# Low parts of the weight tiles: a second ScalarE pass and an adding transfer in place of a VectorE subtraction

## The chip, the core and the metric

The kernel runs on one core of a Trainium2 chip. The core has TensorE (PE; its weight loads are shown as PEld), VectorE (DVE), ScalarE (ACT), GpSimd (POOL) and SyncE (SP), which work side by side and wait for one another through semaphores, and 16 DMA engines that move data between HBM and SBUF. The metric is the device time of one execution in microseconds (us).

## The reference

One inference step of one layer of a hybrid diffusion backbone, in fp32, for 512 latent and 128 context tokens of width 1024. Cut to what matters here:

```python
h = rms_norm(x, norm1_g) * (1.0 + scale1) + shift1
proj = h @ w_in                      # q, k, v, conv, z, x/B/C, dt, gates
y_attn = blocked_attention(...) @ w_attn_o
y_conv = (conv_bg * dwconv_centred(conv_cg * conv_x, conv_w)) @ w_conv_o
y_ssd  = rms_norm(y * silu(z), ssd_norm_g) @ w_ssd_o
out = (g_attn * y_attn + g_conv * y_conv + g_ssd * y_ssd) @ w_merge
x = x + gate1 * out
h = rms_norm(x, norm2_g) * (1.0 + scale2) + shift2
hg, hu = jnp.split(h @ ffn_w1, 2, axis=-1)
x = x + gate2 * ((silu(hg) * hu) @ ffn_w2)
```

Nearly all the arithmetic is products of a token matrix with a weight matrix.

## The kernel before

TensorE multiplies in the rounded format fp32r, which keeps part of an fp32 value. To come close to fp32 every operand X is held as two parts: the high part is X rounded to fp32r, the low part is X minus the high part. A product takes three matmuls: high x high, high x low, low x high.

**Making the parts of a weight tile.** `wraw` (L173) lets SP load up to four blocks of 128 rows by 256 columns, 512 KB, into a raw tile `wr`, of which there are three. `wtiles` (L163) gives a pair `wh`, `wl` out of rings of four each. `split` (L154) then copies the raw tile into `wh` on ACT, which rounds it (L156), and subtracts on DVE, `wl = wr - wh` (L157). A raw tile can be loaded anew when its subtraction is done; `wh` and `wl` can be written anew when TensorE has done its last matmul with the tile that they held before. `wload` (L178) does this for a whole set of 1024 rows in two tiles. Nearly all weight splits are issued with high priority, so that the scheduler of the framework sets them early in the queues of ACT and DVE. Each engine's queue runs in order, as does SP's queue of DMA issues.

**The stages, in order of time.** Start-up and the modulation of the first norm (to 45 us). Attention (45 to 450 us): keys, values and queries by `tblock` (L274), with gate and convolution projections as filling work. Eight groups of the state-space scan (450 to 1043 us): `group_proj` (L746) projects the next group (weights w_x, w_bc, w_z) while `group_scan` (L777) works on the present one; its rows `rw` come back from HBM through SP (L818). The merge of the three branches (1043 to 1270 us): for each pair of 128-column blocks a `wload` of w_ao, w_co or w_so, and `fblock` (L250), 96 matmuls of 320 columns; beside it DVE works off the second modulation (L956), whose rows SP loads. The product with w_mg in two halves of the tokens (L1055), the second norm (`norm_half`, L1080; its power runs on POOL, L282) and the first feed-forward unit by `plain_half` (L1110). From about 1385 us the feed-forward part.

**A feed-forward unit.** `sunit` (L208) computes a 1024 x 256 weight block times the tokens with seven products instead of eight (a Strassen-Winograd scheme). `sload` (L190) loads the block in two raw tiles `r0`, `r1`, forms four sums of quarters on POOL (L197 to L200) in the tiles `ws`, of which there are two, and splits seven quarters into four pairs of `wh`, `wl`. A product is 12 matmuls; between products, ACT copies the first one out of PSUM and DVE adds and subtracts the others (all at L225, through the helper `first`). Twenty such units, two for each column block, alternate with `ff_down` (L1168), which multiplies by the second feed-forward matrix.

**Where the change touches.** `split` stays for the activations and for the narrow w_dt; `wload`, `sload`, `plain_half` (L1113), the load of the first feed-forward unit (L1130), the host's layout of `w_f1` (L1272) and the scratch memory for DMA descriptors (L1285) are changed.

## Time and profile before

| | us |
|---|---|
| three runs, median | 1819.34 |
| three runs, lowest and highest | 1816.97, 1819.56 |
| profiled execution, device time | 1815.66 |
| its span, first to last instruction | 1813.9 |

The profile is of one execution. Its clock of TensorE was granted at 0.993 of full speed over the span. A row of the groups gives line, engine, operation, what it writes and reads (names without buffer numbers), shape and count, then busy time and the mean of one in ns, then the idle time of the engine before these instructions and who ended it. A row of the waits gives who waited for whom: total us, how often, longest. Matmuls overlap each other and the weight loads, so a matmul's own duration (311 ns for 320 columns) is longer than the distance to the next one.

### The profile page before, as it was taken

What the parts mean: (1) busy time and instruction counts of PE and PEld (TensorE: products, weight loads), DVE (VectorE), ACT (ScalarE), POOL (GpSimd) and SP (SyncE); (2) the same over time, 40 slices, a digit from 0 to 9 for tenths busy, and PEclk for the clock granted to TensorE, in tenths of its full rate; (3) what the DMA queues carried; (4) which work ended last, traced back from release to release, by engine and by line L of the source; (5) the groups of instructions that cost most, each with busy time, mean ns of one, the idle gap of its engine ahead of it and who ended that gap; (6) DMA issues with size and microseconds to landing.
All of it is one profiled execution on the core that took longest, in us unless ns stands there. A gap on an engine that the chain in (4) does not pass through costs nothing. (4 is left out here: it accounts for less than half of the span.)

```text
span 1813.9 us, 30158 instructions
## 1 busy us (share of the span) xinstructions
PE 1763.5 (97%) x12104; PEld 1692.3 (93%) x12104; DVE 1203.6 (66%) x2179; ACT 779.6 (43%) x1548; POOL 157.6 (9%) x117
## 2 busy tenths in 40 slices
PE   7999999999999999999999999999988999999999
PEld 3999999999999999999999999999988999999999
DVE  5648545545677677777775478878669666767675
ACT  5554554444455555555555342212345332324240
POOL 0110000000000000000000000000016232232320
PEclk9999999999999999999999999999999999999999
DMA  7312212125243433434334488665531222223222
GB/s 294 108 39 78 69 58 76 68 74 156 75 138 103 144 119 111 140 87 142 119 111 138 131 300 274 216 196 162 190 108 47 82 70 82 74 79 96 67 77 76
DMA packets 110524, 216.50 MB, mean 119 GB/s; under 512 B 9328, under 2 KB 53232, under 8 KB 109360
## 3 DMA queue, kind: packets, MB, share of 16 engines
q1 hardware_dynamic: 110384, 214.58, 36.5%
q8 instruction: 95, 1.56, 0.3%
q14 instruction: 45, 0.37, 0.1%
HBM read 191.05 MB, written 23.49 MB: 118 GB/s over the span
## 5 line engine op out<-in xcount | busy, mean ns | idle before, releaser
L256 PE MATMUL acc<-h,wh 128*128 128x320 f32 x3072 | 582.0, 311 | 3.3 <-DVE s L505 1.0
L256 PEld LDWEIGHTS acc<-h,wh 128*128 128x128 f32 x3072 | 480.7, 188 | 4.7 <-DVE pTl L157 1.6
L157 DVE TENSOR_TENSOR wl<-wr,wh 128x1024 fp32r<-128x1024 f32 (+1 forms) x226 | 279.6, 1238 | 124.9 <-ACT wh L156 115.6
L256 PE MATMUL acc<-h,wl 128*128 128x320 f32 x1536 | 350.4, 309 | 0.9 <-DVE wl L157 0.9
L156 ACT CAST wh<-wr 128x1024 fp32r<-128x1024 f32 (+1 forms) x226 | 224.6, 996 | 282.5 <-PE acc L256 147.4
L256 PE MATMUL acc<-s,wh 128*128 128x320 f32 x1472 | 287.1, 310 | 0.4 <-ACT wh L156 0.4
L256 PEld LDWEIGHTS acc<-h,wl 128*128 128x128 f32 x1536 | 257.0, 188 | 1.4 <-DVE wl L157 1.4
L256 PEld LDWEIGHTS acc<-s,wh 128*128 128x128 f32 x1472 | 234.8, 188 | 1.0 <-ACT wh L156 0.7
L256 PE MATMUL acc<-s,wl 128*128 128x320 f32 x736 | 179.3, 310 | 1.1 <-DVE wl L157 1.1
L246 PE MATMUL mx<-wh,h 128*128 128x256 f32 x560 | 161.6, 289 | 1.7 <-DVE vl L157 1.0
L247 PE MATMUL mx<-wl,h 128*128 128x256 f32 x560 | 159.0, 284 | 0.0
L248 PE MATMUL mx<-wh,h 128*128 128x256 f32 x560 | 158.8, 284 | 0.0
L220 PE MATMUL acc<-s,wh 128*128 128x320 f32 x640 | 148.0, 317 | 5.0 <-ACT s L225 3.0
L256 PEld LDWEIGHTS acc<-s,wl 128*128 128x128 f32 x736 | 126.1, 189 | 2.1 <-DVE wl L157 2.1
L220 PEld LDWEIGHTS acc<-s,wh 128*128 128x128 f32 x640 | 105.6, 188 | 13.1 <-ACT s L225 7.1
L220 PE MATMUL acc<-h,wh 128*128 128x320 f32 x480 | 112.0, 317 | 3.8 <-DVE s L225 2.8
L956 DVE CUSTOM_DVE_ANT_0 jk<-aw,cr 128x512 f32<-128x512 f32 x128 | 88.2, 689 | 34.1 <-DMA aw<-in_ada_dram 32.6
L246 PEld LDWEIGHTS mx<-wh,h 128*128 128x128 f32 x560 | 107.7, 193 | 2.3 <-DVE vl L157 1.2
L825 ACT ACTIVATE ex<-rw,nlc 128x128 f32<-128x128 f32 x320 | 101.8, 391 | 15.4 <-DVE M L827 9.4
L247 PEld LDWEIGHTS mx<-wl,h 128*128 128x128 f32 x560 | 107.9, 193 | 0.0
L248 PEld LDWEIGHTS mx<-wh,h 128*128 128x128 f32 x560 | 107.7, 192 | 0.1
L1052 DVE SCALAR_TENSOR_TENSOR s<-acc,mod,s 128x320 f32<-128x320 f32 (+2 forms) x168 | 65.6, 433 | 61.3 <-PE acc L256 61.1
(267 smaller groups left out, 2612.7 us busy)
## 6 DMA issues: line engine op xcount, KB each, us to landing
wr<-in_w_f_dram SPq DMA_DIRECT2D x64, 512.0 KB, 3.6
rw<-D_a SPq DMA_DIRECT2D x40, 512.0 KB, 5.1
aw<-in_ada_dram SPq DMA_DIRECT2D x64, 256.0 KB, 3.5
wr<-in_w_cv_dram SPq DMA_DIRECT2D x24, 512.0 KB, 3.7
wr<-in_w_gt_dram SPq DMA_DIRECT2D x24, 512.0 KB, 5.0
aw<-in_ada_dram SPq DMA_DIRECT2D x8, 1024.0 KB, 6.7
wr<-in_w_x_dram SPq DMA_DIRECT2D x16, 512.0 KB, 3.9
wr<-in_w_bc_dram SPq DMA_DIRECT2D x16, 512.0 KB, 3.9
```

The source lines that it names most:

```text
L156: act.copy(hi_t, src)
L157: dve.tensor_tensor(lo_t, src, f32(hi_t), op=sub)
L220: pe.matmul(out, y, z, start=not more and i == 0 and j == 0, stop=i == KB // 2 - 1 and j == 2, skip_group_check=True)
L246: pe.matmul(out, l.hi, r.hi, start=start, stop=False)
L247: pe.matmul(out, l.hi, r.lo, start=False, stop=False)
L248: pe.matmul(out, l.lo, r.hi, start=False, stop=stop)
L256: pe.matmul(ps[:, e, :HT], x, y[:, e * HT:(e + 1) * HT], start=first and i == 0 and j == 0, stop=last and i == k - 1 and j == 2)
L825: act.activation(ex[:, d, r, :], rw[:, d, r, :], AF.Exp, bias=nlc[:, c, j:j + 1])
L956: dve.tensor_tensor_reduce(jk, aw, cr[:, s, :], 0.5, 0.0, op0=mult, op1=add, accum_out=mp[:, q, m, s:s + 1])
L1052: dve.scalar_tensor_tensor(dst[:, a:a + n], ps[:, e, a - e * HT:a - e * HT + n], gcol[:, k, s:s + 1], dst[:, a:a + n], op0=mult, op1=add)
```

## The change

A new helper `wsplit` makes both parts of a weight tile: ACT copies the raw tile into `wh` as before, a second ACT pass writes the negative of `wh` into `wl`, and a DMA issued from POOL adds the raw tile onto `wl`. It is used for every weight tile of 256 columns; DVE no longer takes part. The raw tile is read by the DMA, so it comes free when that has landed.

So that the quarters of `w_f1` lie in one piece for the DMA, the host lays that matrix out by quarters, and `sload` and the first feed-forward unit load quarters (`qraw`, `qload`); the numbers in them are the same. The scratch memory for descriptors of DMAs issued by POOL grows from 1024 to 2048.

```diff
+    def wsplit(hi_t, lo_t, src):
+
+        act.copy(hi_t, src)
+        act.mul(lo_t, f32(hi_t), -1.0)
+        pool.dma_start(lo_t, src, accum_op=add)
+
@@ wload
-                split(w.hi, w.lo, raw)
+                (wsplit if n == 256 else split)(w.hi, w.lo, raw)
...
+    def qraw(src, a):
+        t = wp.tile([P, 2, 4, P], F32, tag="wr", name=nm("wr"), bufs=3)
+        nc.sync.dma_start(t, src[:, a])
+        return t
+
+    def qload(src):
+
+        out = []
+        for a in range(2):
+            raw, w = qraw(src, a), wtiles((2, 4, P))
+            with tc.high_priority():
+                wsplit(w.hi, w.lo, raw)
+            out.append(w)
+        return out
+
@@ sload
-        r0, r1 = (wraw(src, a, a + 4).rearrange("p k (m c) -> p m k c", m=2) for a in (0, 4))
+        r0, r1 = qraw(src, 0), qraw(src, 1)
...
-            split(w[0].hi[:, 0], w[0].lo[:, 0], r0[:, 0])
-            split(w[0].hi[:, 1], w[0].lo[:, 1], s24[:, 0])
-            split(w[1].hi, w[1].lo, s31)
-            split(w[2].hi, w[2].lo, r1)
-            split(w[3].hi[:, 0], w[3].lo[:, 0], s24[:, 1])
+            wsplit(w[0].hi[:, 0], w[0].lo[:, 0], r0[:, 0])
+            wsplit(w[0].hi[:, 1], w[0].lo[:, 1], s24[:, 0])
+            wsplit(w[1].hi, w[1].lo, s31)
+            wsplit(w[2].hi, w[2].lo, r1)
+            wsplit(w[3].hi[:, 0], w[3].lo[:, 0], s24[:, 1])
@@ plain_half
-            l, x = w[:, i, m * P:(m + 1) * P], forms[("B11", "B21", "B12", "B22")[2 * e + i // 4]][i % 4]
+            l, x = w[i // 4][:, m, i % 4], forms[("B11", "B21", "B12", "B22")[2 * e + i // 4]][i % 4]
@@ layer_kernel
-    wg, wu = wload(w_f1[0, 0]), wload(w_f1[1, 0])
+    wg, wu = qload(w_f1[0, 0]), qload(w_f1[1, 0])
@@ host
+def _quarters(w):
+
+    t = _wt(w)
+    return t.reshape(*t.shape[:2], 2, 4, 2, P).transpose(0, 1, 2, 4, 3, 5)
...
-        "w_f1": _wt(f1).reshape(2, 11, P, KB, 256),
+        "w_f1": _quarters(f1).reshape(2, 11, P, 2, 2, 4, P),
...
-    nc = bacc.Bacc("TRN2", target_bir_lowering=False, num_devices=1, dynamic_dma_scratch_size=1024)
+    nc = bacc.Bacc("TRN2", target_bir_lowering=False, num_devices=1, dynamic_dma_scratch_size=2048)
```

## The prediction

> **What bounds the kernel now.** I read the page's first two parts, then busy time by stage, then the list of waits.

> ```profile
> span 1813.9 us, 30158 instructions
> PE 1763.5 (97%) x12104; PEld 1692.3 (93%) x12104; DVE 1203.6 (66%) x2179; ACT 779.6 (43%) x1548; POOL 157.6 (9%) x117
> ```

> TensorE is busy 97% of the span: the end is set by the stream of matmuls, and the change leaves their number as it is. What can be won is time in which TensorE stands still for an operand. By stage (columns: stretch, length, busy time and instructions of each engine, granted clock, DMA share, GB/s):

> ```profile
> 0.00:45.00 45.00, 32.24 (x156) 15.61 (x156) 22.62 (x42) 22.46 (x38) 1.38 (x5) 0.92 0.80 296
> 45.00:450.00 405.00, 393.68 (x2871) 385.46 (x2871) 226.49 (x484) 201.76 (x436) 14.35 (x13) 0.99 0.25 80
> 450.00:1043.00 593.00, 593.00 (x4148) 564.38 (x4147) 402.17 (x718) 308.61 (x722) 1.17 (x1) 1.00 0.38 120
> 1043.00:1270.00 227.00, 222.67 (x1509) 220.64 (x1508) 181.31 (x373) 59.09 (x73) 0.00 (x0) 1.00 0.70 230
> 1270.00:1350.00 80.00, 76.85 (x514) 76.31 (x513) 54.49 (x88) 35.94 (x55) 3.12 (x2) 0.98 0.48 161
> 1350.00:1410.00 60.00, 51.52 (x320) 49.02 (x319) 48.07 (x69) 27.92 (x60) 34.70 (x28) 0.94 0.17 49
> 1410.00:1813.90 403.90, 393.51 (x2599) 380.85 (x2597) 268.42 (x407) 123.87 (x168) 102.85 (x68) 1.00 0.25 78
> ```

> The start-up splits no weights before 44.7 us; attention (45 to 450) lacks 11 us, the scan stage (450 to 1043) nothing, the merge of the branches (1043 to 1270) 4, the stage around the second norm 12, the feed-forward part 10. DVE is the fuller helper everywhere from 450 on (80% in the merge, 80% around the norm). Who made TensorE wait (engine, line, who; total us, times, longest):

> ```profile
> PEld acc L220 <- DVE s L225: 8.3, 13, 1.0
> PEld acc L220 <- ACT s L225: 7.1, 19, 0.8
> PEld acc L256 <- DVE wl L157: 3.5, 6, 1.2
> PE acc L220 <- DVE s L225: 4.8, 12, 0.7
> PE acc L220 <- ACT s L225: 3.0, 6, 0.5
> PE acc L256 <- DVE wl L157: 2.0, 4, 0.9
> PEld acc L289 <- POOL rs L282: 6.3, 3, 3.2
> SPq L175 <- DVE wl L157: 971.3, 180, 30.4
> ```

> The first six are the waits that a lighter DVE queue can shorten: the seven-product units of the feed-forward part (L220) wait for subtractions and a copy at L225 that stand in queues behind weight splits, and a few merge tiles wait for the split itself. The loads sum to 8.3 + 7.1 + 3.5 = 18.9 us, the matmuls behind them to 4.8 + 3.0 + 2.0 = 9.8. The gain cannot exceed 19 us, and is near 10 if only what TensorE lost comes back.

> **What is removed and added.** These are the weight splits, by shape:

> ```profile
> L157 DVE TENSOR_TENSOR wl<-wr,wh 128x1024 fp32r<-128x1024 f32 x200 | 258.0, 1291 | 123.9 <-ACT wh L156 114.8 <-PE mx L839 5.5 <-PE acc L620 1.8
> L157 DVE TENSOR_TENSOR wl<-ws,wh 128x512 fp32r<-128x512 f32 x40 | 30.8, 771 | 1.0
> L157 DVE TENSOR_TENSOR wl<-ws,wh 128x1024 fp32r<-128x1024 f32 x20 | 24.5, 1223 | 3.0 <-ACT wh L156 3.0
> L157 DVE TENSOR_TENSOR wl<-wr,wh 128x512 fp32r<-128x512 f32 x24 | 20.8, 866 | 0.0
> L156 ACT CAST wh<-wr 128x1024 fp32r<-128x1024 f32 x200 | 209.0, 1047 | 226.0 <-PE acc L256 124.5 <-issue 30.7 <-PE acc L220 25.8
> L156 ACT CAST wh<-ws 128x512 fp32r<-128x512 f32 x40 | 24.8, 620 | 50.0 <-PE acc L256 24.0 <-PE acc L220 23.9 <-POOL ws L199 2.1
> ```

> DVE loses 258.0 + 30.8 + 24.5 + 20.8 = 334 us (1204 to 870, 48%). ACT gains a second pass, which I price like the first: 220 of 1.05 and 64 of 0.62 = 271 us (780 to 1051, 58%); no stage fills it, the scan stage going from 309 to about 375 of 593 us. POOL gains 284 DMA issues, and the DMA engines 220 x 0.524 + 64 x 0.262 = 132 MB to add. None of these is on the path by its sum. What decides is **latency**: a low part was there 1.2 us after its rounded part; now it comes after a second ACT pass (1.05 us), an issue on POOL and a landing. Call issue plus landing D.

> **The cost D.** No transfer of before is issued by POOL or adds. The nearest rows (size, median us from issue to landing):

> ```profile
> wr<-in_w_f_dram SPq DMA_DIRECT2D x64, 512.0 KB, 3.6
> aw<-in_ada_dram SPq DMA_DIRECT2D x8, 1024.0 KB, 6.7
> wr<-in_w_mg_dram SPq DMA_DIRECT2D x16, 512.0 KB, 4.3
> out_dram<-so SPq DMA_DIRECT2D x8, 256.0 KB, 2.0
> out_dram<-raw SPq DMA_DIRECT2D x1, 128.0 KB, 1.7
> ```

> An addition must read source and destination, so it moves like 1024 KB read. The stores, whose source is SBUF as here, go from 1.7 to 2.0 us for 128 KB more: 0.3 per 128 KB after 1.4, hence 2.6 for 512 KB read once and 3.8 for it read twice. The one row that moves 1024 KB took 6.7, in the crowded start-up. So D lies between 2.6 and 6.7 us; I take 4.8, nearer the SBUF row plus about 1 for an issue that a compute engine makes.

> [...]

> **Where D is covered.** The cover is the time from the end of the rounding to TensorE's first load of that tile's low part. Five places, each a rounding pass and the load that needs it:

> ```profile
> 1491.77 1.05 ACT L156 CAST wh<-ws 128x1024 fp32r<-128x1024 f32 x1 [2.68 <-PE acc L220]
> 1500.01 0.19 PEld L220 LDWEIGHTS acc<-s,wl 128*128 128x128 f32 x1
> 713.54 1.05 ACT L156 CAST wh<-wr 128x1024 fp32r<-128x1024 f32 x1
> 720.73 0.19 PEld L247 LDWEIGHTS mx<-wl,h 128*128 128x128 f32 x1
> 1500.68 1.05 ACT L156 CAST wh<-wr 128x1024 fp32r<-128x1024 f32 x1
> 1507.40 0.33 PEld L256 LDWEIGHTS acc<-s,wl 128*128 128x128 f32 x2
> 44.75 1.04 ACT L156 CAST wh<-wr 128x1024 fp32r<-128x1024 f32 x1
> 50.13 0.19 PEld L247 LDWEIGHTS mx<-wl,h 128*128 128x128 f32 x1
> 1288.97 1.05 ACT L156 CAST wh<-wr 128x1024 fp32r<-128x1024 f32 x1 [1.86 <-PE acc L256]
> 1297.83 0.19 PEld L256 LDWEIGHTS acc<-s,wl 128*128 128x128 f32 x1
> ```

> Less the second pass, what is left for D: second tile of a product unit 1500.01 - 1492.82 - 1.05 = 6.1 us (20 units); second tile of a scan group's z weights 720.73 - 714.59 - 1.05 = 5.1 (8); first tile of an ff_down part 1507.40 - 1501.73 - 1.05 = 4.6 (5); the first key weights 50.13 - 45.79 - 1.05 = 3.3 (once); a merge tile of half a row 1297.83 - 1290.02 - 1.05 = 6.8 (16). Elsewhere the same reading gives more. At D = 4.8 short are ff_down, 0.2 x 5 = 1, and the key weights, 1.5 us.

> **Waits that move.** SP's weight loads wait for the raw tile (971 us in 180 waits); it now comes free at the landing, 1.05 + 4.8 - 1.23 = 4.6 us later. Behind it on SP stand the scan's row loads and the gate stores, which the scan's look-ahead hides, I take 0. The three raw tiles bind in the half-row merge alone: a tile is held 4.3 (load) + 2.1 (two passes) + 4.8 = 11.2 us, a third of that 3.7 a tile, while TensorE eats one in (1303.06 - 1288.97) / 4 = 3.5 us, by these roundings, which TensorE releases:

> ```profile
> 1303.06 1.05 ACT L156 CAST wh<-wr 128x1024 fp32r<-128x1024 f32 x1 [0.60 <-PE acc L256]
> ```

> That is 0.2 x 13 tiles (three are there before) = 2.6 us. On POOL, behind a DMA that waits for ACT, stand the sums of the next unit (L197 to L200) and the power of the norm (L282), for which TensorE already waits 6.3 us; I add 1.

> **Sum.** Of the 9.8 to 18.9 us I take 12 back, since the copies at L225 sit on an ACT queue that gets longer. 12 - 1 - 1.5 - 2.6 - 1 = 6 us. The profiled execution took 1815.7 (span 1813.9), so 1809.7; the three runs have a median of 1819.3, which makes **1813** for a median.

> **Rivals.**

> *The low part lands late (slower).* One mechanism: D above the cover, from about 5.3 us on, where the costs pass the gain of 12. At D = 6.7: units 0.6 x 20 = 12, z tiles 1.6 x 8 = 13, ff_down 2.1 x 5 = 10, key weights 3.4, raw tiles (13.1 / 3 - 3.5) x 13 = 11, power 1: 50 less 12, so +38, 1857. At 5.8 the same sum is 0 + 6 + 6 + 2.5 + 7 + 1 = 22, so +10, 1829. For it: 512 KB loads alone already take 3.6 to 4.3. Against it: SBUF stores land in 2.0.

> *The DMA engines fill in the merge (slower).* They are 0.70 busy there with 230 GB/s, so full at about 329. By the code its 16 loads bring 2 tiles each, 32 x 0.524 = 16.8 MB to add, 0.22 of the stage read once, 0.45 read twice, which makes 1.15 of it: 0.15 x 227 = 34 us at most, some of which prefetch takes: +15, less the gain, 1822 to 1840. From a share of 0.85 without additions on it would be sure.

> [...]

> *ACT takes DVE's place (no change).* Two passes in a row stand before the copy at L225, and its 7.1 us grow as DVE's 8.3 go: 1818 to 1821. For it: ACT already shares these waits. Against it: ACT has 124 of 404 us busy there.

> **How the numbers follow.** Forecast 0.42 (1805 to 1816), late landing 0.29, full DMA engines 0.11, ACT in DVE's place 0.18. The range runs from the ceiling of the gain less the start-up cost, 1819 - 17 = 1802, to 1848, which leaves out late landing near its upper end; the forecast's own range is 1805 to 1816. About 0.2% (3.6 us) is what a measurement of this kernel can tell: faster 0.41, same 0.20, slower 0.39.

> **What would show it.** Right: DVE near 870 us, ACT near 1050; the waits of L220 for L225 down from 18.9 to under 8 with L256's, landing of the adding transfers of 512 KB below 5 us. Late landing: new waits of PEld on a DMA into wl, first in ff_down and the z tiles. Full engines: a DMA share near 1 from 1043 to 1270 and later waits there. ACT's place: L220 <- ACT s L225 above 12. I would be wrong altogether if POOL's issues took several us each, so that its queue, not the landing, set D.

## The result, and the profile after

The changed kernel is slower: 2030.0 us median of four runs (2023.44 to 2039.56) against 1818.15 for the kernel before (1815.62 to 1819.56), a ratio of 1.1171 with a 95% interval of 1.1124 to 1.1219. The forecast was 1813, its range 1802 to 1848. The profiled execution took 2028.74 us; lines have moved by about 21 (L277 was L256, L241 was L220, L246 was L225).

First the page's totals and its rows of DMA queues (packets, MB, share of the 16 engines' span):

```profile
span 2027.0 us, 30864 instructions
PE 1828.0 (90%) x12104; PEld 1750.4 (86%) x12104; DVE 887.3 (44%) x1895; ACT 1028.4 (51%) x1832; POOL 382.7 (19%) x401
q0 software_dynamic: 40896, 132.14, 35.6%
q1 hardware_dynamic: 110384, 214.58, 32.5%
```

The work went where it was meant to go: DVE 887 us (870 forecast), ACT 1028 (1051), 132.14 MB more to move. But the span is 213.1 us longer, and that splits in two: TensorE stands still for 2027.0 - 1828.0 = 199.0 us instead of 1813.9 - 1763.5 = 50.4, which is 148.6 more, and the same 12104 matmuls take 1828.0 - 1763.5 = 64.5 us longer. The additions fill as much of the DMA engines as everything else: 35.6% for 132 MB, 32.5% for 215 MB.

By stage (stretch, length, busy time of PE, PEld, DVE, ACT and POOL, granted clock, DMA share, GB/s), cut at the first instruction on TensorE of each: the scan, the merge, w_mg with the norm and the first unit, the rest of the feed-forward part:

```profile
468.90:1087.60 618.70, 586.20 (x3961) 553.26 (x3960) 317.94 (x638) 356.18 (x771) 55.30 (x64) 0.98 0.64 163
...
1112.70:1391.20 278.50, 240.77 (x1538) 238.00 (x1538) 146.92 (x337) 89.44 (x99) 27.58 (x32) 0.92 0.85 242
1391.20:1518.60 127.40, 101.15 (x603) 97.61 (x601) 54.26 (x105) 68.81 (x117) 40.84 (x42) 0.89 0.73 177
1518.60:2027.00 508.40, 437.39 (x2738) 425.24 (x2736) 154.31 (x309) 228.98 (x303) 201.98 (x197) 0.94 0.73 160
```

Cut in the same way, the kernel before took 568.8, 229.5, 102.0 and 428.6 us there; its merge and its feed-forward part (same columns):

```profile
1053.80:1283.30 229.50, 227.06 (x1538) 225.27 (x1538) 181.65 (x370) 55.11 (x67) 0.00 (x0) 1.00 0.67 219
1385.30:1813.90 428.60, 415.56 (x2737) 401.37 (x2736) 287.80 (x430) 132.94 (x182) 113.54 (x76) 1.00 0.25 78
```

So the scan lost 50 us, the merge 49, the stage around the norm 25 and the feed-forward part 80; attention lost 3. These waits of the changed kernel stand behind it (engine, line, who; total us, times, longest):

```profile
PEld acc L277 <- DMA wl<-wr: 52.0, 17, 8.1
PEld acc L241 <- DMA wl<-ws: 32.9, 11, 4.6
PEld acc L241 <- DMA wl<-wr: 20.9, 11, 4.0
PEld acc L277 <- ACT x L776: 20.9, 6, 4.0
DVE rw L841 <- DMA rw<-D_a: 133.5, 33, 9.8
ACT wh L165 <- POOL ws L220: 94.9, 19, 6.7
```

The first three are TensorE waiting for an adding transfer to land. The last three are indirect: a projection of the scan waits for an ACT copy, DVE waits for the scan's row loads (14.9 us in all before), and the rounding waits for sums on POOL. The rows of the DMA issues (size, median us from issue to landing) show that other loads grew slower too; before, `rw` took 5.1, `w_mg` 4.3:

```profile
wl<-wr POOLq DMA_DIRECT2D x200, 512.0 KB, 5.7
rw<-D_a SPq DMA_DIRECT2D x40, 512.0 KB, 7.0
wl<-ws POOLq DMA_DIRECT2D x40, 256.0 KB, 4.6
wr<-in_w_mg_dram SPq DMA_DIRECT2D x16, 512.0 KB, 6.0
```

### The profile page after: what moved, and what is told of

Its sections match the earlier page's. It is cut to its first block, busy times and chain, and to the rows that moved or that the text cites. A ratio compares the mean times of both kernels' runs of the same rounds, so it can differ in the third digit from the quotient of the medians.

```text
span 2027.0 us, 30864 instructions
## 1 busy us (share of the span) xinstructions
PE 1828.0 (90%) x12104; PEld 1750.4 (86%) x12104; DVE 887.3 (44%) x1895; ACT 1028.4 (51%) x1832; POOL 382.7 (19%) x401
## 3 DMA queue, kind: packets, MB, share of 16 engines
q0 software_dynamic: 40896, 132.14, 35.6%
q1 hardware_dynamic: 110384, 214.58, 32.5%
## 5 line engine op out<-in xcount | busy, mean ns | idle before, releaser
L277 PE MATMUL acc<-h,wh 128*128 128x320 f32 x3072 | 591.4, 315 | 23.3 <-ACT x L776 19.8
L277 PEld LDWEIGHTS acc<-h,wh 128*128 128x128 f32 x3072 | 489.6, 192 | 25.4 <-ACT x L776 20.9
L167 POOL DMA_DIRECT2D wl<-wr x224 | 194.6, 869 | 1390.3 <-ACT wl L166 1281.8
L277 PE MATMUL acc<-h,wl 128*128 128x320 f32 x1536 | 355.6, 313 | 11.1 <-DMA wl<-wr 11.0
L277 PE MATMUL acc<-s,wh 128*128 128x320 f32 x1472 | 296.4, 318 | 5.1 <-ACT wh L165 5.1
L166 ACT ACTIVATE wl<-wh 128x1024 fp32r<-128x1024 f32 (+1 forms) x284 | 271.7, 959 | 5.0
L277 PEld LDWEIGHTS acc<-h,wl 128*128 128x128 f32 x1536 | 261.4, 191 | 12.1 <-DMA wl<-wr 12.1
L277 PEld LDWEIGHTS acc<-s,wh 128*128 128x128 f32 x1472 | 244.2, 196 | 6.1 <-ACT wh L165 5.8
L277 PE MATMUL acc<-s,wl 128*128 128x320 f32 x736 | 185.7, 320 | 36.2 <-DMA wl<-wr 36.2
L277 PEld LDWEIGHTS acc<-s,wl 128*128 128x128 f32 x736 | 131.1, 196 | 39.9 <-DMA wl<-wr 39.9
L241 PE MATMUL acc<-s,wh 128*128 128x320 f32 x640 | 153.3, 329 | 0.0
L241 PE MATMUL acc<-h,wh 128*128 128x320 f32 x480 | 118.4, 334 | 17.8 <-DVE g L246 17.6
L241 PE MATMUL acc<-s,wl 128*128 128x320 f32 x320 | 104.3, 329 | 30.0 <-DMA wl<-ws 30.0
L977 DVE CUSTOM_DVE_ANT_0 jk<-aw,cr 128x512 f32<-128x512 f32 x128 | 88.2, 689 | 85.4 <-DMA aw<-in_ada_dram 83.3
L267 PEld LDWEIGHTS mx<-wh,h 128*128 128x128 f32 x560 | 109.2, 195 | 10.3 <-issue 6.6
L241 PEld LDWEIGHTS acc<-s,wh 128*128 128x128 f32 x640 | 115.4, 203 | 2.7 <-ACT s L246 0.9
## 6 DMA issues: line engine op xcount, KB each, us to landing
wl<-wr POOLq DMA_DIRECT2D x200, 512.0 KB, 5.7
wr<-in_w_f_dram SPq DMA_DIRECT2D x64, 512.0 KB, 4.4
rw<-D_a SPq DMA_DIRECT2D x40, 512.0 KB, 7.0
aw<-in_ada_dram SPq DMA_DIRECT2D x64, 256.0 KB, 4.3
wr<-in_w_cv_dram SPq DMA_DIRECT2D x24, 512.0 KB, 3.9
wr<-in_w_gt_dram SPq DMA_DIRECT2D x24, 512.0 KB, 5.1
wl<-ws POOLq DMA_DIRECT2D x40, 256.0 KB, 4.6
wl<-ws POOLq DMA_DIRECT2D x20, 512.0 KB, 5.6
```

The costliest lines, as they stand in the source:

```text
L166: act.mul(lo_t, f32(hi_t), -1.0)
L167: pool.dma_start(lo_t, src, accum_op=add)
L241: pe.matmul(out, y, z, start=not more and i == 0 and j == 0, stop=i == KB // 2 - 1 and j == 2, skip_group_check=True)
L267: pe.matmul(out, l.hi, r.hi, start=start, stop=False)
L277: pe.matmul(ps[:, e, :HT], x, y[:, e * HT:(e + 1) * HT], start=first and i == 0 and j == 0, stop=last and i == k - 1 and j == 2)
L977: dve.tensor_tensor_reduce(jk, aw, cr[:, s, :], 0.5, 0.0, op0=mult, op1=add, accum_out=mp[:, q, m, s:s + 1])
```

## The experiments

The theories at the start: the low parts land too late for TensorE (*late landing*); the additions take the DMA engines from other transfers (*traffic*); a queue in order, SP's or POOL's, holds other work behind a landing. Eighteen kernels ran. Stage lengths are read from their traces in us: the scan from its first transposition to its last, the merge from its first matmul to the first one with w_mg, w_mg from there to the first matmul of `plain_half`, and the product units from the first matmul to the last (`ff_down` lies between them). In the column "before" stands the old kernel's time on the same chip. No_add and att_only ran in three rounds, every other experiment once; a stage that an edit left alone still moved by up to some 6 us from one kernel to the next.

| run | time | before | scan | merge | w_mg | units |
|---|---|---|---|---|---|---|
| before | 1815.7 | | 568.8 | 229.6 | 63.1 | 382.5 |
| after | 2028.7 | 1818.2 | 618.8 | 278.6 | 82.9 | 462.2 |
| two_pass | 1834.8 | 1823.6 | 570.0 | 229.7 | 63.3 | 384.5 |
| no_add | 1814.2 | 1817.1 | 570.0 | 230.9 | 59.5 | 376.5 |
| traffic | 1933.5 | 1823.6 | 574.5 | 283.2 | 77.8 | 400.6 |
| eighth | 1899.8 | 1823.6 | 610.1 | 240.5 | 64.7 | 405.6 |
| plain_copy | 1891.5 | 1818.4 | 585.5 | 258.7 | 70.2 | 402.0 |
| merge_dve | 1964.3 | 1814.4 | 624.2 | 229.8 | 63.0 | 463.8 |
| ring5 | 2025.7 | 1823.6 | 616.7 | 274.6 | 83.3 | 452.1 |
| sums4 | 2041.1 | 1817.1 | 618.8 | 283.2 | 79.8 | 467.4 |
| raw5 | 2020.3 | 1817.1 | 615.2 | 283.0 | 72.8 | 460.2 |
| sums_dve | 1997.0 | 1814.4 | 621.5 | 278.8 | 83.1 | 418.5 |
| deep | 1995.7 | 1814.4 | 613.7 | 281.0 | 74.8 | 437.4 |
| rw_own_queue | 2024.5 | 1817.1 | 620.0 | 280.3 | 80.7 | 460.4 |
| rows3 | 2034.0 | 1814.4 | 617.0 | 281.6 | 82.7 | 460.2 |
| eighth_own | 1873.4 | 1816.4 | 581.6 | 244.0 | 63.8 | 405.1 |
| ex_first | 2050.4 | 1816.4 | 631.9 | 284.9 | 80.5 | 460.9 |
| ex_first_own3 | 2048.6 | 1816.4 | 628.1 | 282.7 | 81.6 | 464.9 |
| all_fix | 1938.8 | 1816.4 | 632.3 | 231.1 | 64.5 | 416.1 |
| att_only | 1821.3 | 1818.4 | 568.8 | 227.2 | 64.5 | 382.3 |

**The ACT pass and the lighter DVE queue.**

```diff
# two_pass
-        pool.dma_start(lo_t, src, accum_op=add)
+        dve.tensor_tensor(lo_t, src, f32(lo_t), op=add)
# no_add
-        pool.dma_start(lo_t, src, accum_op=add)
```

> The ACT pass alone: low part = negative of the rounded part (ACT), then an addition on DVE in place of the adding transfer; no transfer, DVE as heavy as before. Late landing (each tile waits for the landing) and traffic (the DMA engines are taken from other transfers) both expect the time of before plus at most the 1.05 us by which a low part comes later: 1818 to 1835 us, ACT near 1030 us busy, DVE near 1200. If ACT's second pass were the cost: 1950 us or more.

> The lighter DVE queue by itself: both ACT passes stay, the adding transfers are left out altogether, so low parts are only the negatives of the rounded parts. DVE near 870 us, ACT near 1030, no waits on a landing. If the gain of 12 us that the prediction counted is there, with ACT's second pass hidden: 1800 to 1810. If ACT takes DVE's place: 1816 to 1825. If the second pass costs what the two-pass run lost (11 us) and the lighter DVE gives nothing: 1826 to 1835.

The second pass alone cost 11 us in one run, most of it before the scan, which began at 475.7 us (464.1 before); scan, merge and w_mg are within 1.2 us of before, the units 2 longer. The kernel without the addition has the same second pass, and its ratio is 0.9977 (0.9964 to 0.9991) in three rounds: a gain of about 4 us. It lies in the units (6.0 us) and around w_mg (3.6). But the wait that was to shrink most did not: TensorE's loads still wait 8.2 us for DVE's subtractions in the units (8.3 before), though DVE splits no weight there, and 4.5 us for ACT's copies (7.1 before):

```profile
PEld acc L240 <- DVE s L245: 8.2, 10, 1.2
...
PEld acc L240 <- ACT s L245: 4.5, 19, 0.3
```

The run without the addition also shows that the new order of the queues is harmless as such: the framework's scheduler puts 169 of ACT's 1548 other instructions in another place than before, most of them in the scan, which takes 570.0 us all the same.

**Traffic, waits, and the addition itself.**

```diff
# traffic (junk: two scrap tiles, filled with zeros once; raw = slot(mo, "raw", bufs=3) makes room)
-        act.mul(lo_t, f32(hi_t), -1.0)
-        pool.dma_start(lo_t, src, accum_op=add)
+        dve.tensor_tensor(lo_t, src, f32(hi_t), op=sub)
+        j = junk[len(junked) % 2][:, :int(np.prod(src.shape[1:]))]
...
+        pool.dma_start(j.rearrange(...), f32(hi_t), accum_op=add)
# eighth
-        pool.dma_start(lo_t, src, accum_op=add)
+        k = (slice(None),) + (0,) * (len(src.shape) - 2) + (slice(0, P),)
+        pool.dma_start(lo_t[k], src[k], accum_op=add)
# plain_copy
-        pool.dma_start(lo_t, src, accum_op=add)
+        pool.dma_start(f32(lo_t), src)
```

> The traffic alone: low parts by DVE as before, and beside each an adding transfer of the same size from the rounded tile into a scrap tile that nobody reads, issued by POOL after the rounding. Bytes, queue and POOL order as in the changed kernel; TensorE and the raw tiles wait for no landing. Late landing expects 1818 to 1850 us. Traffic expects 1950 us or more, with the merge of the branches as slow as in the changed kernel (about 278 us against 229). Both at work: in between, with the merge slow and the feed-forward part close to before.

> The same waits with little traffic: each adding transfer moves only the first 128 columns of each partition's row (an eighth of a tile of 512 KB, a quarter of one of 256 KB); the rest of the low part stays the negative of the rounded part. Issue on POOL 0.87 us as before, landing expected at 2 to 3 us in place of 5.7. If the cost is the size of the transfer, by its landing or its traffic: below 1840 us, with a gain of up to 15 us under 1818 possible. If it is the chain as such (POOL's queue, issue, two passes): above 1900.

> The change with a plain copy of the raw tile in place of the addition, same bytes written, same queue, same waits (so that the low part is the raw tile itself). If the addition reads two sources and that is what fills the engines: the queue's share per MB falls by a third to a half (35.6% of 2027 us for 132 MB in the changed kernel), the 512 KB transfer lands in under 5 us, and the merge falls under 260 us, in all under 1985. If POOL's queue is slow by itself: share and merge as in the changed kernel, above 2010.

Neither simple theory holds alone. Traffic for whose landing neither TensorE nor a raw tile waits cost 110 us, half of it in the merge: 283.2 us, no less than in the changed kernel. The waits with a seventh of the bytes (18.63 MB) cost 76, more than half of it in the scan, though landings took 2.6 us, under every cover that the prediction had listed. And with a copy of the same bytes in place of the addition the loss is 73 us (1891.5 against 1818.4), where the addition loses 211 (2028.7 against 1818.2). Its rows of queue and issues:

```profile
q0 software_dynamic: 36800, 132.14, 17.9%
wl<-wr POOLq DMA_DIRECT2D x200, 512.0 KB, 3.7
```

By the spans, the copies took 0.179 x 1889.7 = 338 us of all 16 engines, the additions 0.356 x 2027.0 = 722 for the same 132.14 MB: for each 512 KB (252 of them) 1.34 and 2.86 us. The landing went from 5.7 to 3.7. So the additions took 722 / 338 = 2.1 times the engines' time of copies of the same size. The copy differs in one thing more: it writes fp32, where the addition writes fp32r. That is not the cause, since the additions of the run with traffic go from fp32 to fp32 and took 0.385 x 1931.7 = 744 us:

```profile
q0 software_dynamic: 40896, 132.14, 38.5%
```

**The merge.**

```diff
# merge_dve: wload gets dma=True
-                (wsplit if n == 256 else split)(w.hi, w.lo, raw)
+                (wsplit if dma and n == 256 else split)(w.hi, w.lo, raw)
-        w = wload(wo[mt])
+        w = wload(wo[mt], dma=False)
-            w = wload(w_mg[mt])
+            w = wload(w_mg[mt], dma=False)
```

> The change everywhere but in the merge of the branches and the products with w_mg, whose low parts are subtracted by DVE as before. If full DMA engines are what the merge loses: 229 to 240 us there (279 in the changed kernel) and 63 to 67 for w_mg (83), scan and feed-forward part as slow as in the changed kernel, in all 1945 to 1970. If the loss there comes with the lower clock or a backlog from the scan: above 255 in the merge.

Both stages are back to before within 0.2 us, and scan and units are within 6 us of the changed kernel. The merge as these kernels had it, the run with traffic alone first, then the run with DVE's splits in it (columns as above):

```profile
1082.00:1365.00 283.00, 243.56 (x1537) 238.23 (x1536) 180.84 (x369) 54.51 (x65) 26.73 (x31) 0.93 0.84 237
```

```profile
1117.00:1347.00 230.00, 228.62 (x1540) 227.05 (x1540) 181.22 (x370) 54.92 (x66) 0.00 (x0) 0.99 0.67 217
```

The engines' work in the stage before was 0.67 x 229.5 = 154 us; 32 additions of 2.86 us are 92 more, 246 us in a stage of 229.5. It stretched until the share was 0.84 to 0.85. That is an average: cut at the middle of its matmuls, the merge of the changed kernel ran at 0.94 and then at 0.77:

```profile
1112.70:1255.70 143.00, 122.18 (x771) 120.99 (x771) 78.98 (x183) 48.37 (x54) 13.46 (x16) 0.91 0.94 276
1255.70:1391.20 135.50, 118.59 (x769) 117.02 (x768) 67.94 (x155) 41.07 (x45) 14.12 (x17) 0.92 0.77 206
```

Before, the halves took 112.7 us (share 0.81) and 116.8 (0.54). So 30 of the 49 us were lost while the engines were nearly full, 19 while they had room; and plain copies, with a share of 0.77 over their merge, still cost 29. The additions' traffic is shown to be enough for the loss of the merge. That full engines are all of it is not shown.

Who waits does not matter: with traffic alone it is DVE's subtraction that comes late, because the weights do, by the waits of that stage:

```profile
PEld acc L285 <- DVE wl L171: 40.5, 16, 7.6
...
ACT wh L170 <- DMA wr<-in_w_so_dram: 28.4, 4, 12.5
```

**The product units.**

```diff
# ring5, sums4, raw5, deep: raw = slot(mo, "raw", bufs=3) in place of slot(ph, ...) makes room, and
# ring5: wh, wl   bufs=4 -> 5
# sums4: ws       bufs=2 -> 4
# raw5:  wr       bufs=3 -> 5
# deep:  ws in the feed-forward pool, bufs=4; wr bufs=4; ph bufs=27 -> 26
# sums_dve
-            pool.tensor_tensor(s31[:, 1], r0[:, 1], r1[:, 1], op=add)
+            dve.tensor_tensor(s31[:, 1], r0[:, 1], r1[:, 1], op=add)
...
```

> The change with a fifth pair of weight tiles in the ring of rounded and low parts (the scrap of the merge's raw loads moves to a pool that closes before the feed-forward part, to make room). A tile's cover in the feed-forward part grows by two products, 3.5 us. Late landing expects the feed-forward part's 80 us to fall to under 25, 1975 us or less in all. Traffic expects nothing there: above 2010.

> The change with four tiles for the sums of the product units in place of two (same move to make room). The sums of the next unit then need not wait for the landing of this unit's adding transfers. If that loop sets the feed-forward part: 462 falls to 430 or less, in all 1995 or less, other stages as in the changed kernel. If traffic or the raw tiles set it: within 10 us of the changed kernel.

> The change with five raw weight tiles in place of three (the scrap of the merge's raw loads moves to a pool that closes before the feed-forward part). SP then blocks later. If the held raw tile is what delays SP: scan stage under 590 and the feed-forward part under 430 (462 after), in all under 1980; the merge stays slow (its engines are full), 270 or more. If landing and sums alone set the feed-forward part: above 455 there.

> The change with both rings of the product units deepened at once: four tiles for sums (two before) and four raw tiles (three before), each alone having moved nothing. If the units run in a loop that passes through the landings of both rings: the feed-forward part falls from 462 to 430 or less. If the transfers' own time (traffic) sets it: above 450. The scan stage keeps its 610 to 620, the merge its 270 or more.

> The change with the sums of the product units computed by DVE in place of POOL, whose queue then holds the adding transfers alone. If sums that wait on POOL behind transfers set the feed-forward part: 462 falls to 435 or less. If the loop through landing, sums tiles and raw tiles sets it: 450 to 465, in all within 12 us of the changed kernel.

One deeper ring alone moved the units by -10, +5 and -2 us, so none of the three rings sets the pace by itself. Raw tiles and sums tiles deepened together gave 25 of the 80 us, the sums off POOL 44; but a sum took 1.29 us on POOL, and additions of the same form on DVE take 0.68 (128x512 in fp32, L848 of the changed kernel), so what part of the 44 is the order of POOL's queue and what part the shorter sums stays open. The chain of waits of the changed kernel between 1560 and 1640 us shows why one deeper ring is not enough (start, length, what; only the longer parts of one turn):

```profile
1603.79 5.32 DMA wl<-ws
...
1609.27 1.29 POOL ws L220
...
1610.64 1.30 POOL ws L221
...
1612.11 3.31 DMA wl<-wr
...
1615.56 6.25 DMA wr<-in_w_f_dram
...
1624.47 5.69 DMA wl<-ws
```

It is a loop. The landing of an addition frees the sums tile; only then does POOL form the next unit's sums, the next transfer stands behind them on POOL, its landing frees a raw tile, only then does SP load weights for the unit after, and they are summed again. This turn, with two landings, a load and the sums, took 1624.47 - 1603.79 = 20.7 us. In the kernel before, TensorE began one unit 13.8 us after another where no `ff_down` stood between them (1482.2 and 1496.0 us); the work of `ff_down` comes in one piece of 27 us for every four units. A cover counted for one tile does not see a loop. With the sums on DVE 36 us of the loss are left; TensorE's largest stop there, 21 us in all, is for landings of `wl<-ws`.

**The scan.**

```diff
# rw_own_queue
-                nc.sync.dma_start(rw.rearrange("p d r i -> p (d r) i"),
+                nc.scalar.dma_start(rw.rearrange("p d r i -> p (d r) i"),
# rows3
-                rw = gp.tile([P, 2, HPG, P], F32, tag="rw", name=nm("rw"))
+                rw = gp.tile([P, 2, HPG, P], F32, tag="rw", name=nm("rw"), bufs=3)
# ex_first
-                        act.activation(ex[:, d, r, :], rw[:, d, r, :], AF.Exp, bias=nlc[:, c, j:j + 1])
+                        with tc.high_priority():
+                            act.activation(ex[:, d, r, :], rw[:, d, r, :], AF.Exp, bias=nlc[:, c, j:j + 1])
# eighth_own: eighth with rw_own_queue; ex_first_own3: all three
```

> The change with one edit: the scan's row loads are issued from ACT's queue, so that they no longer stand behind weight loads on SP that wait for a raw tile. If SP's order is what costs the scan stage its 50 us (569 before, 619 after): scan stage 570 to 590, in all 1985 to 2000. If it is traffic or the landing of the low parts: scan above 610, in all 2020 or more. The issues themselves take time on ACT, which could cost up to 10 us.

> The change with three row tiles in the scan in place of two, so that a row load may be issued one chunk earlier. In the changed kernel the exponentials that free a row tile stand later on ACT, and the load then lands 7.0 us after its issue (5.1 before). If these late rows are what TensorE loses in the scan: 570 to 590 us there (619 in the changed kernel, 569 before), in all 1980 to 2002. If the low parts or ACT itself set the scan: above 605, in all above 2010.

> The run with an eighth of the traffic, with the scan's row loads issued from ACT's queue. There the rows stood on SP behind a weight load that waited for a landing. If SP's order is the scan's cost where traffic is small: scan 570 to 585 us (610 in the run with an eighth, 569 before), in all 1860 to 1875. If the order of the exponentials on ACT alone does it: still above 600.

> The change with one edit: the scan's exponentials have the same high priority as the weight passes, so that they stand on ACT before the second passes again and free the row tiles earlier. If the order on ACT is the scan's cost: 570 to 590 us there (619 in the changed kernel), in all 1980 to 2002. If late landing and traffic cost it whatever the order: above 605.

> The same with, in addition, the row loads on ACT's queue and three row tiles, so that a row load waits neither for the exponentials of the chunk before nor for SP. If lateness of the rows is the whole of the scan's cost, by whatever causes: 570 to 585 us there, in all 1975 to 1995. If the low parts themselves land too late for TensorE in the scan: above 600.

This is one of the scan's six long stops in the changed kernel, by the timeline (start, length, instruction, in brackets the wait before it):

```profile
545.50 1.05 ACT L166 ACTIVATE wl<-wh 128x1024 fp32r<-128x1024 f32 x1
545.78 0.33 SPq L181 DMA_DIRECT2D wr<-in_w_bc_dram  x1
546.90 0.89 POOL L167 DMA_DIRECT2D wl<-wr  x1 [3.39 <-ACT yF L884]
547.42 1.59 ACT L846 ACTIVATE ex<-rw,nlc 128x128 f32<-128x128 f32 x5
548.22 0.33 SPq L181 DMA_DIRECT2D wr<-in_w_gt_dram  x1
549.16 0.75 SPq L839 DMA_DIRECT2D rw<-D_a  x1
558.66 1.23 DVE L841 TENSOR_TENSOR rw<-rw,cst 128x1024 f32<-128x1024 f32 x1 [9.76 <-DMA rw<-D_a]
560.13 1.00 DVE L532 SCALAR_TENSOR_TENSOR x<-s,cw,x 128x511 f32<-128x511 f32 x2
...
569.91 0.87 ACT L776 ACTIVATE x<-acc,cw 128x640 f32<-128x640 f32 x1
570.84 1.44 PE L277 MATMUL acc<-h,wh 128*128 128x320 f32 x4 [3.82 <-ACT x L776]
```

The exponentials free the row tile; they now stand behind second passes on ACT. The row load follows them, lands some 9 us later beside an adding transfer, two weight loads and two stores of results, and holds DVE up. DVE's convolution comes late, then ACT's, then TensorE's next `acc` (3.82 us). With the load on ACT's queue the issue no longer waits for SP, but the landing stays as slow:

```profile
546.50 0.37 ACTq L839 DMA_DIRECT2D rw<-D_a  x1
```

```profile
556.08 1.23 DVE L841 TENSOR_TENSOR rw<-rw,cst 128x1024 f32<-128x1024 f32 x1 [9.71 <-DMA rw<-D_a]
```

Where traffic is small, SP's order is the larger cause: the same edit on the run with an eighth took the scan from 610.1 to 581.6. With the exponentials put first the rows come in time, and the low parts no longer do, by the waits of that run's scan:

```profile
DVE rw L841 <- DMA rw<-D_a: 26.2, 15, 3.1
...
PE mx L268 <- DMA wl<-wr: 22.4, 7, 4.1
...
PE acc L277 <- DMA wl<-wr: 8.0, 6, 1.8
```

The wait for rows fell from 124 to 26 us in the scan, TensorE's waits for landings rose from 6 to 30, and the scan got longer by 13 us. So three things share one margin: ACT's order, SP's order and the landings. No edit that keeps whole additions gave the scan back, a third row tile (617.0) as little as the others; plain copies, which land in 3.7 us, cost it only 17. By the stage rows 32.5 of the 50 us are stops of TensorE (19.8 of them the six long ones) and 17.4 are slower matmuls. How the 50 us split between the three causes stays open.

**All together, and one stage alone.** all_fix joins merge_dve, sums_dve, deep and ex_first_own3; att_only keeps the change for w_k, w_v, w_q and w_cv and splits all else on DVE.

> All edits that showed an effect or may show one, together: merge and w_mg split by DVE; sums of the product units on DVE, four tiles for sums and four raw tiles; in the scan the exponentials first, rows on ACT's queue, three row tiles. If the loss is the sum of three places: 229 for the merge, 63 for w_mg, 390 to 420 for the feed-forward part, 570 to 590 for the scan, in all 1820 to 1870. If something common to all stages (the clock, POOL's issues) costs as well: above 1890.

> The change only for the weights of keys, values, queries and convolution (36 of the 284 transfers), which attention computes with; all other low parts by DVE as before. The DMA engines are a quarter busy there and the changed kernel lost only 2 us between the first product and the scan. If a transfer costs only where it is uncovered or the engines are full: 1812 to 1824. If each transfer costs something by itself (213 us over 284 is 0.75 each): 1840 or more.

The first is still 122 us slower than before. Merge and w_mg are within 1.5 us of before, the units came down to 416.1, the scan did not (632.3). Scan and units, which keep the additions, hold 97 of the 122 us, so a cost common to all stages is not needed. The second, with 36 of the 284 transfers, gives 1.0019 (1.0008 to 1.0030): some 3 us. There the engines were a quarter busy (0.25 before) and the covers long: a transfer cost next to nothing, and brought nothing. No version with the transfers beat the kernel before.

## Why the prediction was wrong

**The step that failed** is "None of these is on the path by its sum. What decides is latency": the forecast set the 132 MB of additions, and the queues that they pass through, at next to nothing. Traffic for whose landing TensorE does not wait cost 110 us, the waits with a seventh of the bytes 76. The parts follow.

**What bounds the kernel: right; the gain of 12 us: too large.** Without the transfers the units and w_mg gained 9.6 us, and about 4 remain of it in the whole. The largest wait that a lighter DVE was to shorten, 8.3 us for its subtractions at L225, stayed at 8.2.

**Work removed and added: right** for DVE, ACT and the bytes. POOL's issue took 0.87 us (869 ns in the row at the end), so the mishap that was named, several us each, did not come. Yet POOL was on the path in the units, with the sums that stand in its queue between the transfers: in place of the term "On POOL, behind a DMA that waits for ACT, stand the sums of the next unit", priced with the norm's power at 1 us, taking the sums off POOL gave 44.

**D: too low, but not the failure.** 4.8 us was taken, of which about 1 for an issue by a compute engine was the author's estimate (POOL's took 0.87); landings took 5.7, and an issue starts 0.35 us after the pass (565.03 + 1.04 to 566.42 in the trace), so 6.05. The rival's own sum gives 0 + 8 + 7 + 3 + 8 + 1 = 27 us at that value, 15 after the gain of 12, or 1834. An eighth of the bytes, landing in 2.6 us, should have gained by the same sum, and lost 76. What failed is the way of counting: a cover for each tile, each taken alone, with every other transfer at its old duration.

**"Behind it on SP stand the scan's row loads and the gate stores, which the scan's look-ahead hides, I take 0": wrong.** DVE's wait for rows rose from 14.9 to 133.5 us, and the long stop that was followed back above began with a late row. SP's order is shown to cost 28 us where traffic is small (610.1 to 581.6). With the full additions, rows that came in time did not shorten the scan, so what the rows cost there stays open. A look-ahead of two row tiles was no cover, and three were none either.

**"The raw tiles bind in the half-row merge alone", 2.6 us: wrong in its place.** They bind in the units' loop, together with the sums tiles; neither ring alone shows it. Five raw tiles left the merge at 283.0 us and took 10 of the 20 us off w_mg (72.8).

**Full DMA engines in the merge: the right rival, mis-sized.** The share worked out for additions that read twice, 0.45, was near the 92 / 229.5 = 0.40 measured. That an addition reads twice no run shows; what they show is 2.1 times the engines' time of a copy. The prediction then cut 34 us to 15 for prefetch and gave it 11 in 100. The merge lost 49. By the measured price, 246 us of transfers at a share of 1, full engines alone would have cost 16; the sum counted the stage as one, though its first half was at 0.81 before and its second at 0.54. More raw tiles to prefetch into did not help.

**Left out: the clock.** 64.5 of the 213 us are matmuls that ran slower, with the mean granted clock at 0.953 (0.993 before). In the traces of the two kernels the recorded clock is either full or half (1.00 or 0.50), so the means say that it was half for 191 and 26 us; by the same traces TensorE was at work in 153 and 21 of them, and half of the difference, 66 us, covers the 64.5. What starts it can be read after three stops of TensorE, of 3.82, 3.31 and 2.54 us (the first ended at 570.84, the second at 649.67, the third at 964.03). The windows follow the grid on which the clock changes: in both traces any two changes lie a whole number of steps of 3.413 us apart (columns as above; PE's busy time is the second figure, the clock the third from the end):

```profile
566.08:569.50 3.42, 0.94 (x6) 0.52 (x4) 0.00 (x0) 3.42 (x8) 0.87 (x1) 1.00 0.52 101
569.50:572.91 3.41, 2.08 (x8) 2.08 (x9) 2.09 (x5) 3.41 (x6) 0.86 (x1) 0.50 0.74 130
...
644.59:648.00 3.41, 1.78 (x9) 1.03 (x7) 0.00 (x0) 3.41 (x9) 0.87 (x1) 1.00 0.42 80
648.00:651.41 3.41, 1.74 (x12) 1.74 (x13) 1.75 (x4) 3.41 (x6) 0.86 (x1) 1.00 0.74 130
...
962.03:965.44 3.41, 1.41 (x9) 1.41 (x10) 1.42 (x3) 3.41 (x7) 0.86 (x1) 1.00 0.76 129
965.44:968.86 3.42, 3.42 (x15) 3.42 (x14) 3.42 (x9) 2.60 (x5) 0.86 (x1) 0.50 0.94 211
```

A step with 0.94 or 1.41 us of work was followed by half clock, two steps with 1.78 and 1.74 were not: the stop of 3.31 us fell half into each. The traces of the two kernels, counted from their first change of clock on, agree: of the steps at full clock, all 34 in which TensorE was busy under 40% were followed by half clock, 5 of the 10 in which it was busy 40 to 50%, and 3 of the 1009 in which it was busy half of the time or more.

The third stop shows that 2.54 us can be enough, if 2.0 of them fall into one step. In the 4 us after the first stop, at a clock of 0.50, TensorE worked on 15 matmuls, in those after the second, at 1.00, on 27:

```profile
570.84:574.84 4.00, 4.00 (x15) 4.00 (x16) 4.00 (x9) 4.00 (x7) 1.24 (x2) 0.50 0.81 122
649.67:653.67 4.00, 4.00 (x27) 4.00 (x28) 4.00 (x9) 4.00 (x7) 1.25 (x2) 1.00 0.84 137
```

By the clock of 0.50 a step of 3.413 us then does an estimated 1.7 us less work, so such a stop costs more than its own length, and the prediction's sums had none of that.

**ACT in DVE's place: did not come** as described; TensorE's loads waited 0.9 us for ACT's copies in the units, in place of 7.1. In the scan ACT's new order delays the rows, but without the additions the same order cost nothing there (570.0).

## What to carry to other kernels

A step that moves from a compute engine to the DMA engines must be priced in the engines' time, stage by stage, an addition at what it took here, 2.86 us of all 16 engines for 512 KB, 2.1 times a copy: a merge at 0.67 on average, whose first half was at 0.81, did not take 0.40 more without growing, whoever waited (229.6 us to 278.6, and to 283.2 with traffic alone). Where a transfer's landing frees buffers, follow the loop through all rings and queues that the buffer passes, since a cover counted for one tile holds only if nothing else in the turn gets later. And a gain bounded at 1% is a poor reason to give an operand of every matmul a latency six times as long (1.05 + 0.35 + 5.7 = 7.1 us after the rounding, in place of 1.2).

## What the hardware showed that was not expected

- An adding transfer from SBUF to SBUF issued by POOL took 2.86 us of all 16 engines per 512 KB (183 GB/s), a plain copy on the same queue 1.34 (391 GB/s); rounding to fp32r had no part in it (744 us for all additions from fp32 to fp32, 722 to fp32r). POOL was busy 869 ns for one issue of the former and 535 of the latter, by the groups of the changed kernel and of the run with copies:

```profile
L167 POOL DMA_DIRECT2D wl<-wr x224 | 194.6, 869 | 1390.3 <-ACT wl L166 1281.8 <-ACT yF L884 35.0 <-ACT s L1088 16.6
```

```profile
L167 POOL DMA_DIRECT2D wl<-wr x224 | 119.8, 535 | 1361.4 <-ACT wl L166 1248.1 <-ACT yF L884 37.7 <-DMA wr<-in_w_co_dram 16.4
```
